# A hybrid decoder layer on one core: other costs in the kernel's own scheduler, a sixth side bank, and output rows turned in one operation

## The chip, the core and the metric

The kernel runs on one core of a Trainium2 chip. TensorE (PE) multiplies, VectorE (DVE) and ScalarE (ACT) work element by element, GpSimd (POOL) does a little, and SyncE (SP) issues nearly all DMAs. Every engine works through its own queue in order. A matmul adds into one of the eight PSUM banks, 128 partitions of 512 floats each. The time is device microseconds of one execution; what counts is the median of several runs.

## The reference

One layer for 256 new tokens of a prompt and 64 tokens of eight running sequences, all in float32:

```python
proj = x @ w_in                       # 2048 -> 16392 columns
(ml_q, ml_k, ml_v, ml_i, ml_f, ml_o, hg_q, hg_f, hg_i, hg_g, gate_a, gate_b) = split(proj)
h, C, n, m = mlstm(q, k, v, ig, lf, C0, n0, m0)      # 4 heads, state 256 x 512 each
branch_a = layernorm(h) * ml_norm_g * sigmoid(ml_o)
o, S = hgrn2(hq, log f, 1 - f, i, S0)                # 8 heads, state 128 x 256 each
branch_b = rmsnorm(o) * hg_norm_g * silu(hg_g)
merged = sigmoid(gate_a) * (branch_a @ w_branch_a) + sigmoid(gate_b) * (branch_b @ w_branch_b)
x1 = layernorm(alpha * x + merged @ w_out)
y = layernorm(alpha * x1 + relu(x1 @ w_up) ** 2 @ w_down)
```

The outputs are y for both groups and the new states of all heads (C, n, m of the mLSTM, S of the HGRN2).

## The kernel before

**The main stream.** All weight products are cut into tiles of 128 output columns for all 320 tokens. A tile sums 16 blocks of 128 rows (k). Each float32 factor is split into a high and a low part, so one k is three matmuls, which this document calls a step: high x high, high x low, low x high. A tile is 16 steps, 48 matmuls. The weights come in units of half a tile (eight blocks, 128 x 1024 floats): SP loads one (`wr<-wt`), ACT copies its high part (`wh`), DVE takes the low part (`wl`, in `prep`, L497). The list of tiles (`tile_list`) fixes the order of the main stream: for each of the four mLSTM heads v, k, q and two gates (the gates are `ga` and `gb`, the merge gates); four more gates; for each of the eight HGRN2 heads two gates, f, q and two tiles of i; 16 tiles of the mLSTM output gate (`o`), four gates, then 16 pairs of HGRN2 output gate and branch projection (`hg`, `wa`), `wb`, `wo`, and the feed-forward part (`up`, `dn`).

**The side work.** The heads' recurrences are written as generators (`m_E`, `m_S`, `m_V`, `m_num`, `m_sample`, `m_update`, ... for the mLSTM, `h_scan`, `h_i`, `h_state`, `h_out`, ... for the HGRN2). Each yields one instruction at a time with its engine and its cost, or waits for an event, or takes or returns a buffer from a pool. Their matmuls ("side matmuls") stand between the main ones.

**What sets the order.** The class `Sched` keeps an account: a time for every engine, counted in nanoseconds from given costs, not measured. After each step of the main stream (`run_main`) it lets the generators run as far as the account permits. An instruction may be written down if its input is ready by the account, plus a latency: LAT if it comes from another engine, SAME if it comes from the same one. A side matmul needs PE_LAT (450) more and is written only when the account's TensorE time has reached that point. So the numbers of the account decide where each instruction stands in its engine's queue; the time on the chip decides whether it then has to wait. A DMA counts 620 on SP, then 1,500 plus its bytes at 380 a nanosecond plus 600 (`transfer`). `until` lets the account's time pass until a condition holds.

**Banks.** Three of the eight banks serve the main stream (`mbank`), one the gates' first product and then, like the other four, the side work (`sbank`). A tile's evacuation (`ev_...`) returns its bank after its first reading; for gates and the `o` and `hf` tiles that reading is a DVE operation in `sigmoid` (L1309), for the others an ACT copy.

**Lines the text speaks of.** L356 is the helper of all matmuls that are not transposes, L350 that of all ACT operations, L359 that of all DMAs of SP. L1156 and L1159 are the turning transposes of DVE (`turn`, 24 for each head), L1631 that of the HGRN2's output rows, L1090 that of the mLSTM's. `h_i` turns i, splits it (L1488, tile `rh`) and multiplies it by a spreading matrix (`rh,ra`, two side matmuls of 128 x 256). `h_state` stacks k in two parts (`stack`, L987) and has TensorE transpose the result (L1530), from which ACT makes four copies of 32 partitions. `m_sample` multiplies the mLSTM states, loaded from HBM (`rx<-C`, `f<-C`, 16 loads of 256 KB for each head), in two groups of eight matmuls a head: eight groups in all; `m_update` and `m_store` change the states and store them (`Cs`). L1049 is the end of the mLSTM's layernorm (`ln_post`), whose rows TensorE transposes at L1212. `m_CP` stores k (`kD`, four DMAs of 32-partition pieces) and v (`vD`, 1 MB) for later use.

Of the kernel before, what the change touches and what calls it, by code (L numbers as in the profile page):

```python
# [20 lines left out]
TOK = 320  # L21
# [4 lines left out]
LN_SH = 62  # L26
# [93 lines left out]
V_MLG, V_HGG, V_G1, V_B1, V_G2, V_B2, V_LB, V_BI, V_BF, V_END = 0, 16, 32, 48, 64, 80, 96, 112, 113, 114  # L120


LAT = 140.0
SAME = 100.0
PE_LAT = 450.0


# [16 lines left out]
class Sched:  # L144
# [24 lines left out]
    def step(self, c, now):  # L169
        if c.req is None:  # L170
            try:
                c.req = c.gen.send(c.send)
            except StopIteration:
                c.done = True
                return False
            c.send = None
        kind = c.req[0]
        if kind == "wait":
            for e in c.req[1]:
                if e.t is None:  # L180
                    return False
            c.ready = max([c.ready] + [e.t for e in c.req[1]])
            c.eng = None
        elif kind == "acq":
            pool, n = c.req[1], c.req[2]
            if len(pool.free) < n:
                return False
            pool.free.sort(key=lambda x: x[0])
            got, pool.free = pool.free[:n], pool.free[n:]
            c.ready = max([c.ready] + [x[0] for x in got])  # L190
            c.eng = None
            c.send = got[0][1] if n == 1 else [x[1] for x in got]
        elif kind == "rel":
            c.req[1].free.append((c.ready, c.req[2]))
        elif kind == "set":
            c.req[1].t = c.ready
        else:
            _, cost, fn, *after = c.req
            r = max(after[0]) if after else c.ready
            if c.eng != kind or after:  # L200
                r += LAT
            elif kind in ("act", "dve"):
                r += SAME
            if kind == "pe":
# [62 lines left out]


def dve_t(n):
    return 155.0 + 1.07 * n  # L270


def pe_f(n, m=128):
# [40 lines left out]
class Program:  # L314
# [163 lines left out]
    def prep(self, must=False):  # L478

        u = self.next_prep  # L480
        if u >= len(UNITS) or not self.hl_free:
            return False
        now = self.s.t["pe"]
        if must:
            self.s.until(lambda: u in self.raw_at)
        elif u not in self.raw_at:
            return False
        if not must and (self.raw_at[u] > now + 200 or self.hl_free[0][0] > now + 200 or self.s.t["dve"] > now + 1200):
            return False
# [4 lines left out]
        e = s.use("act", max(at, self.raw_at[u]) + LAT, act(1024))  # L494
        self.A(hi, raw)
        e = s.use("dve", e + LAT, dve(1024))
# [85 lines left out]
    def before(self, i, t):  # L582
        s = self.s
        kind, h, c = t[:3]
        if kind == "mv" and c == 0:
            s.until(lambda: self.vr.free and self.qk.free)
            self.m_start(h)
            self.vr.free.sort(key=lambda x: x[0])
            self.mh[h]["vr"] = self.vr.free.pop(0)[1]
        elif kind == "hf":  # L590
            s.until(lambda: self.hs.free)
            if h == 0:
                s.spawn(self.m_after(), 0)
            self.h_start(h)
        elif kind == "o" and h == 0:
            s.until(lambda: all(m["end"].t is not None for m in self.mh))
        elif kind == "hg" and h == 0:
            s.until(lambda: all(m["end"].t is not None for m in self.hh))
            self.carve_m()
            self.carve_b()  # L600
            B = self.Part(self.f2)
            for pool in (self.sg, self.sg, self.sr, self.ld, self.ld, self.ld):
                pool.free.append((s.t["pe"], B(320)))
        if kind in ("o", "wa", "hg", "wb"):
            s.spawn(self.fetch(kind, h), 1)
        elif kind == "mk" and h == 0 and c == 0:
            self.load_ev.t = s.t["pe"]
            self.dma(self.lmask, self.d["lmask"])
        elif kind == "wo" and h == 0:
            s.until(lambda: len(self.sbank.free) >= 5)  # L610
            self.mbank.free += self.sbank.free[:3]
            del self.sbank.free[:3]
            self.hl_free += [(s.t["pe"], x) for x in self.wx[:4]]
            R = self.Part(self.wxv[4].rearrange("p x s v -> p (x s v)"))
            self.lns = [R.three(2, TOK) for _ in range(3)]
            s.spawn(self.ln_x(), 1)
        elif kind == "dn" and c == 3 and h == 0:
# [302 lines left out]
    def m_S(self, h):  # L920
# [20 lines left out]
        yield ("act", act(128), lambda: self.A(ss[64:128, 0:128], E[64:128, 384:512]))  # L941
# [361 lines left out]
    def sigmoid(self, p, out, r, free=()):  # L1303
# [9 lines left out]
        yield ("act", act(TOK), lambda: self.A(r, out, AF.Ln, scale=2.0 ** -LN_SH, bias=self.ln_b))  # L1313
        yield ("act", act(TOK), lambda: self.A(r, r, AF.Exp, scale=-1.0, bias=self.exp_b))
        yield ("dve", dve(TOK), lambda: v.scalar_tensor_tensor(out, out, 1.0, r, ALU.add, ALU.mult))  # L1315
        yield ("dve", dve(TOK), lambda: v.scalar_tensor_tensor(out, out, 2.0, r, ALU.subtract, ALU.mult))  # L1316

    def ev_hf(self, h, c, b):
# [5 lines left out]
        yield ("act", act(TOK), lambda: self.A(u, f, AF.Identity, scale=-1.0, bias=self.one))  # L1324
        yield post(m["fd"])

    def ev_hq(self, h, c, b):
# [109 lines left out]
    def h_lag(self, b, at):  # L1437
        v = self.nc.vector
        a4 = at[:, 0:TOK].rearrange("p (b r) -> p b r", r=4)
        for d in (0, 2, 1, 3):  # L1440
# [4 lines left out]
            yield ("dve", dve(n, True), lambda: v.copy_predicated(  # L1445
                a4[:, :, d:4], block(self.lmask[:, M_LAG[d]:M_LAG[d] + n]), block(x[:, lo:lo + n])))
            if d > 1:
                yield rel(self.sbank, x)
# [1 line left out]
    def h_put(self, b, at, B):  # L1450
# [3 lines left out]
        elif B >= 32:  # L1454
            for j in range(64 // B):
                for i in range(2):
                    lo, c = 64 * j + B * i, 128 * i + 64 * j
                    yield ("act", act(B, True), lambda: self.A(
                        at[64 * j:64 * j + B, c + B:c + 2 * B], b[lo:lo + B, c // 2:c // 2 + B]))
        else:  # L1460
            T = TOK if B == 4 else NP_
# [51 lines left out]
    def h_state(self, h):  # L1513
# [17 lines left out]
        yield rel(self.hstg, st)  # L1531
        for x in range(4):
            r = slice(32 * x, 32 * x + 32)
            yield ("act", act(256, True), lambda: self.A(kst[r, x], b[r, 0:256].rearrange("p (g k) -> p g k", g=2)))
        yield rel(self.sbank, b)
        ob = yield acq(self.sbank)
        m["ob2"] = ob
# [77 lines left out]
    def h_out(self, h):  # L1615
# [11 lines left out]
        for i in range(2):  # L1627
            yield from self.rms(b[:, 256 * i:256 * i + 256], on[:, i, :], 128)
        yield rel(self.sbank, b)
        for i in range(2):  # L1630
            yield ("dve", dve_t(256), lambda: v.transpose(on[:, i, :], on[:, i, :]))  # L1631
# [59 lines left out]
    def ev_o(self, j, c, b):  # L1691
# [5 lines left out]
        x = yield from self.fetched("o", j)  # L1697
        yield ("dve", dve(TOK, ptr=1), lambda: v.scalar_tensor_tensor(g, g, self.vec[:, V_MLG + j:V_MLG + j + 1], x, ALU.mult, ALU.mult))  # L1698
        yield rel(self.ld, x)
        yield from self.split(g, self.bah[:, j, :], self.bal[:, j, :])  # L1700
        yield rel(self.sg, g)
        yield post(self.ba_ev[j])
# [386 lines left out]
```

## Time and profile before

| | |
|---|---|
| median of 3 runs | 2305.03 us (2302.9 to 2306.02) |
| profiled execution | 2302.73 us |
| its span | 2300.8 us |
| granted TensorE clock | 0.999 |
| busy share PE / DVE / ACT / POOL | 100% / 63% / 45% / 1% |
| moved by DMA | 424.94 MB, mean 185 GB/s |

The page puts 69% of the chain that ended last down to TensorE. The ends of matmuls are modelled: a main matmul of 320 columns is shown as 0.31 us long, though the next one starts about 0.15 us after it. A gap shorter than that overlap is not shown as idle. Where TensorE waits for a moment, the starts of consecutive matmuls tell more than the busy time. A name like `rx<-C` is output from input; numbers of buffers are left out.

### The profile page before, as it was taken

What the parts mean: (1) busy time and instruction counts of PE and PEld (TensorE: products, weight loads), DVE (VectorE), ACT (ScalarE), POOL (GpSimd) and SP (SyncE); (2) the same over time, 40 slices, a digit from 0 to 9 for tenths busy, and PEclk for the clock granted to TensorE, in tenths of its full rate; (3) what the DMA queues carried; (4) which work ended last, traced back from release to release, by engine and by line L of the source; (5) the groups of instructions that cost most, each with busy time, mean ns of one, the idle gap of its engine ahead of it and who ended that gap; (6) DMA issues with size and microseconds to landing.
All of it is one profiled execution on the core that took longest, in us unless ns stands there. A gap on an engine that the chain in (4) does not pass through costs nothing.

```text
span 2300.8 us, 38921 instructions
## 1 busy us (share of the span) xinstructions
PE 2289.6 (100%) x15592; PEld 2246.1 (98%) x15592; DVE 1458.9 (63%) x2634; ACT 1036.6 (45%) x1653; POOL 13.5 (1%) x37
## 2 busy tenths in 40 slices
PE   9999999999999999999999999999999999999998
PEld 9999899999999999999999999999999999999998
DVE  6786786788888886555555767654444444444455
ACT  5443445455555565444433446533433343234334
POOL 0000000000000000000000000000000000000000
PEclk9999999999999999999999999999999999999999
DMA  7667977755565564555545644444444444444475
GB/s 284 211 186 259 295 250 229 259 176 185 191 207 187 166 198 167 180 174 170 176 172 175 214 163 147 147 147 149 154 147 150 152 147 153 149 147 154 149 228 193
DMA packets 214574, 424.94 MB, mean 185 GB/s; under 512 B 83572, under 2 KB 110068, under 8 KB 213368
## 3 DMA queue, kind: packets, MB, share of 16 engines
q1 hardware_dynamic: 209512, 415.97, 53.7%
q0 software_dynamic: 4736, 6.29, 1.0%
q8 instruction: 122, 2.00, 0.3%
q14 instruction: 60, 0.49, 0.1%
q10 hardware_dynamic: 144, 0.20, 0.0%
HBM read 371.48 MB, written 50.90 MB: 184 GB/s over the span
## 4 chain that ended last, share of the span: by engine, by line
PE 69%; DVE 3%; ACT 1%; issue 0%; ACTq 0%; DVEq 0%
PE bank L356 69%; DVE wl L497 1%; ACT wh L350 0%; DVE f L1156 0%; DVE f L1445 0%; ACT f L350 0%; DVE f3m L1973 0%; DVE f3m L1980 0%; ACT f3m L350 0%; DVE f L1159 0%; DVE f L1315 0%; DVE f L1316 0%; DVE f L1631 0%; DVE f L1698 0%; DVE f L1309 0%
## 5 line engine op out<-in xcount | busy, mean ns | idle before, releaser
L356 PE MATMUL bank<-xh,wh 128*128 128x320 f32 (+1 forms) x2504 | 794.6, 318 | 0.0
L356 PE MATMUL bank<-xh,wl 128*128 128x320 f32 (+1 forms) x2504 | 774.8, 310 | 0.0
L356 PE MATMUL bank<-xl,wh 128*128 128x320 f32 (+1 forms) x2504 | 772.2, 309 | 0.0
L497 DVE TENSOR_TENSOR wl<-wr,wh 128x1024 fp32r<-128x1024 f32 x440 | 538.7, 1224 | 361.4 <-ACT wh L350 358.3
L350 ACT ACTIVATE wh<-wr 128x1024 fp32r<-128x1024 f32 x440 | 465.4, 1058 | 524.7 <-PE bank L356 495.6
L356 PEld LDWEIGHTS bank<-xh,wh 128*128 128x128 f32 x2504 | 472.0, 189 | 17.2 <-issue 15.3
L356 PEld LDWEIGHTS bank<-xl,wh 128*128 128x128 f32 x2504 | 471.5, 188 | 3.3
L356 PEld LDWEIGHTS bank<-xh,wl 128*128 128x128 f32 x2504 | 471.8, 189 | 0.2 <-DVE wl L497 0.2
L497 DVE TENSOR_TENSOR bb<-wr,bb 128x1024 fp32r<-128x1024 f32 x162 | 198.5, 1225 | 193.7 <-ACT bb L350 193.5
L350 ACT ACTIVATE bb<-wr 128x1024 fp32r<-128x1024 f32 x162 | 171.6, 1059 | 294.6 <-PE bank L356 277.5
L356 PE MATMUL bank<-ra,wh 128*128 128x320 f32 x1008 | 275.9, 309 | 0.7 <-DVE ra L1672 0.7
L356 PE MATMUL bank<-ra,bb 128*128 128x320 f32 x1096 | 255.2, 309 | 0.0
L356 PE MATMUL bank<-xh,bb 128*128 128x320 f32 (+1 forms) x1136 | 253.8, 309 | 0.0
L356 PE MATMUL bank<-rxb,bb 128*128 128x320 f32 x1088 | 249.0, 309 | 0.0
L356 PEld LDWEIGHTS bank<-xh,bb 128*128 128x128 f32 x1136 | 191.0, 188 | 0.0
L356 PE MATMUL bank<-rxb,wh 128*128 128x320 f32 x608 | 187.5, 308 | 0.0
L356 PE MATMUL bank<-rxb,wl 128*128 128x320 f32 x608 | 187.5, 308 | 0.0
L356 PEld LDWEIGHTS bank<-ra,bb 128*128 128x128 f32 x1096 | 184.9, 187 | 0.0
L356 PEld LDWEIGHTS bank<-rxb,bb 128*128 128x128 f32 x1088 | 184.2, 187 | 0.0
L356 PEld LDWEIGHTS bank<-ra,wh 128*128 128x128 f32 x1008 | 180.9, 187 | 0.9 <-DVE ra L1672 0.9
L356 PE MATMUL bank<-xl,bb 128*128 128x320 f32 (+1 forms) x568 | 175.5, 309 | 0.0
L356 PE MATMUL bank<-bb,wh 128*128 128x320 f32 (+1 forms) x536 | 119.0, 313 | 0.0
(259 smaller groups left out, 2244.4 us busy)
## 6 DMA issues: line engine op xcount, KB each, us to landing
wr<-wt SPq DMA_DIRECT2D x602, 512.0 KB, 3.3
rx<-C SPq DMA_DIRECT2D x34, 256.0 KB, 5.6
Cs<-rx SPq DMA_DIRECT2D x34, 256.0 KB, 4.8
f<-C SPq DMA_DIRECT2D x30, 256.0 KB, 5.5
Cs<-f SPq DMA_DIRECT2D x30, 256.0 KB, 4.1
f<-first SPq DMA_DIRECT2D x6, 704.0 KB, 9.6
vD<-ra SPq DMA_DIRECT2D x4, 1024.0 KB, 5.2
f<-S SPq DMA_DIRECT2D x8, 512.0 KB, 5.0
```

Of the source, the lines that this page charges most:

```text
L350: return self.nc.scalar.activation(out, in_, func, **kw)
L356: self.nc.tensor.matmul(*a, **kw)
L497: self.V().tensor_tensor(lo, raw, hi.bitcast(F32), ALU.subtract)
```

## The change

LAT falls from 140 to 130. SAME, 100 for ACT and DVE, becomes 127 for ACT and 113 for DVE. A result of TensorE counts 200 until another engine can use it (PE_OUT) instead of LAT. A DVE transpose of n elements counts 295 + 1.05 n instead of 155 + 1.07 n. An ACT copy from or to part of the partitions counts 122 more (PART), at four places. ACT operations with a pointer operand count 93 more at three places. The masked copies of `h_lag`, 398, 315, 231 and 148 before, get fixed costs of 415, 385, 320 and 155. The weight split counts 10 to 20 more.

From the tile `mk` of the first head on, one main bank goes to the side work, which then has six; before the first `hg` tile it goes back. In `h_out` one transpose of 512 columns takes the place of two of 256. In `ev_o` the tiles from the eighth on wait in the account for the last HGRN2 head's attention matrix (`aT`), those from the thirteenth on for its states (`sdone`), ahead of their split.

```diff
-LAT = 140.0
-SAME = 100.0
+LAT = 130.0
+SAME = dict(act=127.0, dve=113.0)
+PE_OUT = 200.0
+PART = 122.0
...
             r = max(after[0]) if after else c.ready
-            if c.eng != kind or after:
+            if c.eng == "pe" and kind != "pe" and not after:
+                r += PE_OUT
+            elif c.eng != kind or after:
                 r += LAT
-            elif kind in ("act", "dve"):
-                r += SAME
+            elif kind in SAME:
+                r += SAME[kind]
...
 def dve_t(n):
-    return 155.0 + 1.07 * n
+    return 295.0 + 1.05 * n
...
+            self.mbank.free.append(self.sbank.free.pop())
             B = self.Part(self.f2)
...
         elif kind == "mk" and h == 0 and c == 0:
+            s.until(lambda: self.mbank.free)
+            self.sbank.free.append(self.mbank.free.pop())
             self.load_ev.t = s.t["pe"]
...
-            yield ("act", act(256, True), lambda: self.A(kst[r, x], b[r, 0:256].rearrange("p (g k) -> p g k", g=2)))
+            yield ("act", act(256, True) + PART, lambda: self.A(kst[r, x], b[r, 0:256].rearrange("p (g k) -> p g k", g=2)))
...
-        for i in range(2):
-            yield ("dve", dve_t(256), lambda: v.transpose(on[:, i, :], on[:, i, :]))
+        yield ("dve", dve_t(512), lambda: v.transpose(on[:, 0:2, :], on[:, 0:2, :]))
...
         yield rel(self.ld, x)
+        if j > 6:
+            yield wait(self.hh[HH - 1]["aT" if j < 12 else "sdone"])
         yield from self.split(g, self.bah[:, j, :], self.bal[:, j, :])
```

The main stream is the same, step for step, and so are the 681 side matmuls; what moves is where they stand. Two places show it. Lines are numbered four to eight higher in the new kernel: L497, L987, L1156, L1159, L1418, L1419 are now L501, L994, L1163, L1166, L1425, L1426.

First DVE's queue in the fourth HGRN2 head, before: from one weight split to the end of the stacking (L987), with the turning of i (L1156) and the norm of the head before (L1664, L1056) between them.

```order
L497 TENSOR_TENSOR wl<-wr,wh 128x1024
L1419 TENSOR_TENSOR f_75<-f_75 128x40
L1156 STREAM_TRANSPOSE f_76<-f_75 32x4x32
L1466 COPY_PREDICATED f_75<-lmask,bank_88 128x40x4
L1156 STREAM_TRANSPOSE f_76<-f_75 32x4x32
L1664 TENSOR_SCALAR misc<-misc 128x1
L1056 TENSOR_SCALAR misc<-misc 128x1
L1156 STREAM_TRANSPOSE f_76<-f_75 32x4x32
L987 TENSOR_TENSOR f_76<-f_75,f_76 128x16x8
```

The same stretch now, from the split of the same unit to the stacking of the same head:

```order
L501 TENSOR_TENSOR wl<-wr,wh 128x1024
L1425 TENSOR_TENSOR f_75<-f_75 128x16x8
L1166 STREAM_TRANSPOSE f_76<-f_75 32x2x32
L994 TENSOR_TENSOR f_76<-f_75,f_76 128x16x8
L1426 TENSOR_TENSOR f_75<-f_75 128x16
```

Seven rows stood between the split and the stacking, now two do; the transposes of TensorE that read the result (L1530) stand at the 1,163rd step before and at the 1,161st now.

Then SP's queue ahead of the fifth group of state matmuls (the third mLSTM head's first). `rx<-C` loads states, `Cs` stores them, `vD` and `kD` are the stores of `m_CP`, `gaD` that of a gate. Before:

```order
L359 DMA gaD_160<-f_76 128x320
L359 DMA Cs<-rx 128x512
L359 DMA vD_114<-ra 128x2048
L359 DMA wr<-wt 128x1024
L359 DMA Cs<-rx 128x512
L359 DMA rx<-C 128x512
L359 DMA Cs<-rx 128x512
L359 DMA rx<-C 128x512
```

Now:

```order
L363 DMA Cs<-rx 128x512
L363 DMA rx<-C 128x512
L363 DMA wr<-wt 128x1024
L363 DMA rx<-C 128x512
L363 DMA Cs<-rx 128x512 x2
L363 DMA wr<-wt 128x1024
L363 DMA rx<-C 128x512 x2
L363 DMA gaD_159<-f_76 128x320
```

The 1 MB store of v no longer stands close ahead of the group's last two loads. Ahead of the third group it is now so with kD, which before stood farther off:

```order
L363 DMA gaD_158<-f_76 128x320
L363 DMA kD_109<-ra 32x32x32
L363 DMA Cs<-rx 128x512
L363 DMA rx<-C 128x512
L363 DMA vD_113<-ra 128x2048
```

Here the `rx<-C` is the group's last load, behind the last of kD's four stores. All eight groups, in both versions, stand on TensorE within 50 steps of each other's place.

More of the change, by code (lines that the diff above doesn't have):

```diff
@@ L493, in prep @@
         s = self.s
-        e = s.use("act", max(at, self.raw_at[u]) + LAT, act(1024))
+        e = s.use("act", max(at, self.raw_at[u]) + LAT, act(1048))
         self.A(hi, raw)
-        e = s.use("dve", e + LAT, dve(1024))
+        e = s.use("dve", e + LAT, dve(1034))
         self.V().tensor_tensor(lo, raw, hi.bitcast(F32), ALU.subtract)
@@ L940, in m_S @@
         yield ("act", act(384), lambda: self.A(sh, E[:, 0:384]))
[L941 removed]
+        yield ("act", act(128) + PART, lambda: self.A(ss[64:128, 0:128], E[64:128, 384:512]))
         yield ("dve", dve(384), lambda: v.tensor_tensor(sl, E[:, 0:384], f(sh), ALU.subtract))
@@ L1312, in sigmoid @@
         yield ("act", act(TOK), lambda: self.A(out, out, AF.Exp))
-        yield ("act", act(TOK), lambda: self.A(r, out, AF.Ln, scale=2.0 ** -LN_SH, bias=self.ln_b))
-        yield ("act", act(TOK), lambda: self.A(r, r, AF.Exp, scale=-1.0, bias=self.exp_b))
+        yield ("act", act(TOK, False, 1), lambda: self.A(r, out, AF.Ln, scale=2.0 ** -LN_SH, bias=self.ln_b))
+        yield ("act", act(TOK, False, 1), lambda: self.A(r, r, AF.Exp, scale=-1.0, bias=self.exp_b))
         yield ("dve", dve(TOK), lambda: v.scalar_tensor_tensor(out, out, 1.0, r, ALU.add, ALU.mult))
@@ L1323, in ev_hf @@
         yield ("dve", dve(TOK, mode=2), lambda: v.tensor_scalar(f, u, l1, lb, ALU.mult, ALU.add))
-        yield ("act", act(TOK), lambda: self.A(u, f, AF.Identity, scale=-1.0, bias=self.one))
+        yield ("act", act(TOK, False, 1), lambda: self.A(u, f, AF.Identity, scale=-1.0, bias=self.one))
         yield post(m["fd"])
@@ L1444, in h_lag @@
             block = lambda y: y.rearrange("p (b r) -> p b r", r=4 - d)
-            yield ("dve", dve(n, True), lambda: v.copy_predicated(
+            yield ("dve", (415.0, 385.0, 320.0, 155.0)[d], lambda: v.copy_predicated(
                 a4[:, :, d:4], block(self.lmask[:, M_LAG[d]:M_LAG[d] + n]), block(x[:, lo:lo + n])))
@@ L1457, in h_put @@
                     lo, c = 64 * j + B * i, 128 * i + 64 * j
-                    yield ("act", act(B, True), lambda: self.A(
+                    yield ("act", act(B, True) + PART, lambda: self.A(
                         at[64 * j:64 * j + B, c + B:c + 2 * B], b[lo:lo + B, c // 2:c // 2 + B]))
```

## The prediction

> **What bounds the kernel now.** I read the page first, then the windows by stage, the waits of TensorE and its timeline around each wait. The page says that TensorE has work all the time:
>
> ```profile
> span 2300.8 us, 38921 instructions
> PE 2289.6 (100%) x15592; PEld 2246.1 (98%) x15592; DVE 1458.9 (63%) x2634; ACT 1036.6 (45%) x1653; POOL 13.5 (1%) x37
> ```
>
> This profiled execution took 2302.73 us, 1.9 more than its span and 2.3 less than the median of the three runs, 2305.03; the sum is made against 2302.73 and carried over to the median as a difference. The windows (PE busy and its matmuls in brackets, then weight loads, DVE, ACT, POOL, granted clock, DMA share, GB/s) give the pace:
>
> ```profile
> 30.00:430.00 400.00, 399.07 (x2690) 371.86 (x2689) 306.09 (x620) 179.27 (x293) 0.00 (x0) 1.00 0.75 245
> 430.00:830.00 400.00, 397.37 (x2781) 386.69 (x2781) 339.54 (x899) 224.17 (x490) 4.74 (x13) 1.00 0.59 190
> 830.00:2277.00 1447.00, 1446.34 (x9853) 1445.61 (x9852) 781.29 (x1042) 599.20 (x802) 5.90 (x8) 1.00 0.48 163
> ```
>
> From 830 to 2277 us a matmul starts every 1447/9853 = 0.147 us at full clock: nothing but fewer matmuls helps there. The first two windows hold the mLSTM and HGRN2 heads, whose side matmuls go between the main ones. The change removes no matmul, so all it can win or lose is TensorE's waiting. The waits (total, times, longest):
>
> ```profile
> PE bank L1530 <- DVE f L987: 1.5, 3, 0.7
> PE bank L356 <- DVE rh L1488: 1.1, 2, 0.6
> PE bank L356 <- POOL ones L640: 1.0, 1, 1.0
> PE bank L1212 <- DVE f L1049: 0.7, 1, 0.7
> PE bank L356 <- DVE ra L1672: 0.7, 1, 0.7
> PE bank L356 <- DMA rx<-C: 0.2, 1, 0.2
> ```
>
> L640 is the start, L1672 lies at 1493 us in the feed-forward part. The other four rows, seven waits, lie in the two windows of the heads. They cost more than is printed, because a matmul counts as busy for 0.31 us but the next starts after 0.147. The timeline of TensorE shows it; the first three rows have a wait, the last three the same matmul without one:
>
> ```profile
> 603.36 0.30 PE L356 MATMUL bank<-xh,wl 128*128 128x320 f32 x1
> 604.33 0.33 PE L1530 MATMUL bank<-cst,f 128*128 128x128 f32 x1 [0.67 <-DVE f L987]
> 604.42 0.39 PE L356 MATMUL bank<-xh,wh 128*128 128x320 f32 x1
> ...
> 605.23 0.31 PE L356 MATMUL bank<-xh,wl 128*128 128x320 f32 x1
> 605.38 0.27 PE L1530 MATMUL bank<-cst,f 128*128 128x128 f32 x1
> 605.41 0.39 PE L356 MATMUL bank<-xh,wh 128*128 128x320 f32 x1
> ```
>
> From main matmul to main matmul it is 1.06 us against 0.18: the 0.67 cost 0.88. So the six waits for DVE, 1.5 + 1.1 + 0.7 = 3.3 printed, cost 3.3 + 6 x 0.21 = 4.6 us. Groups of eight matmuls on the mLSTM states, loaded just ahead of them, differ in the same way:
>
> ```profile
> 232.13 0.31 PE L356 MATMUL bank<-xh,wl 128*128 128x320 f32 x1
> ...
> 234.22 0.42 PE L356 MATMUL bank<-xh,wh 128*128 128x320 f32 x1
> ...
> 265.80 0.31 PE L356 MATMUL bank<-xh,wl 128*128 128x320 f32 x1
> ...
> 268.18 1.05 PE L356 MATMUL bank<-rx,f 128*32 128x512 f32 x2 [0.22 <-DMA rx<-C]
> ...
> 269.15 0.41 PE L356 MATMUL bank<-xh,wh 128*128 128x320 f32 x1
> ...
> 179.83 0.31 PE L356 MATMUL bank<-xh,wl 128*128 128x320 f32 x1
> ...
> 182.72 0.41 PE L356 MATMUL bank<-xh,wh 128*128 128x320 f32 x1
> ...
> 814.72 0.31 PE L356 MATMUL bank<-xh,wl 128*128 128x320 f32 x1
> ...
> 815.13 0.31 PE L356 MATMUL bank<-xh,wh 128*128 128x320 f32 x1
> ...
> 816.10 0.31 PE L356 MATMUL bank<-xh,wl 128*128 128x320 f32 x1
> ...
> 816.37 0.31 PE L356 MATMUL bank<-xh,wh 128*128 128x320 f32 x1
> ```
>
> A group without a wait takes 2.09 us, the one with the printed wait 3.35 (1.26 lost), the one at 180 us 2.89 (0.80 lost, not printed). There are seven such unprinted losses, from the 0.80 here to 0.14 at 814.72 (0.41 against the 0.27 at 816.10 around the same side matmul, one for L1488's tile), together 2.4 us: 1.25 on two state groups, 1.15 on five waits for DVE or ACT. In all the heads lose 5.75 us to computing that comes late and 2.5 to states that come late: 8.25 us, 0.36% of the time. That is all there is to win.
>
> **The change part by part.** A difference under 0.2%, 4.6 us, is about what a measurement of this kernel cannot tell from none.
>
> *The numbers of the account.* They move side work, and no engine gets or loses an instruction by them. TensorE waited at 604.33 for L987, which stood in DVE's queue behind transposes:
>
> ```profile
> 602.27 0.31 DVE L1156 STREAM_TRANSPOSE f<-f 32x128 f32<-32x128 f32 x1
> 602.59 0.33 DVE L1466 COPY_PREDICATED f<-lmask,bank 128x160 f32<-128x160 uint8 x1
> ...
> 603.99 0.29 DVE L987 TENSOR_TENSOR f<-f,f 128x128 fp32r<-128x128 f32 x1
> ```
>
> A transpose of 128 takes the queue 0.32 us there; the old account says 155 + 1.07 x 128 = 292 ns, the new one 429. By groups:
>
> ```profile
> L1156 DVE STREAM_TRANSPOSE f<-f 32x128 f32<-32x128 f32 x96 | 29.0, 303 | 2.3
> L1631 DVE STREAM_TRANSPOSE f<-f 128x256 f32<-128x256 f32 x16 | 7.0, 435 | 0.0
> L1090 DVE STREAM_TRANSPOSE f<-f 128x512 f32<-128x512 f32 x8 | 5.7, 709 | 0.2
> L350 ACT ACTIVATE ra<-bank 32x256 fp32r<-32x256 f32 x32 | 12.0, 374 | 5.5 <-PE bank L1530 5.1
> ```
>
> The old account was short by little in each and by much in sum: a head's 24 turning transposes, and 264 ns for each of four partial copies that take 374. The new one is long instead (429, 564 and 833 for 303, 435 and 709; 386 for 374), about 3.3 us more for a head's turning, while the longest wait for DVE cost some 0.9 (0.7 printed + 0.21). DVE will so be ahead of the account, not behind. The order shows it at head 3: of seven rows between a split and L987 two are left, which at 0.2 to 0.33 a row is some 1.3 us earlier, while its transposes on TensorE stay within two steps of their place. The gain is between 0 (the waits only move) and 5.75. I take 4.6: the six printed waits go, and the five small ones, no longer than the account's own steps, come back elsewhere.
>
> *Side work earlier, then later.* Counted along the main matmuls, mLSTM's side work moves 20 to 50 steps earlier (a step is three matmuls, 0.44 us) and the last HGRN2 heads' 20 to 130 later; the 681 side matmuls are the same. With them move, on SP's queue, the loads and stores of states and the small stores; POOL's order is as before. The later heads end at the 1,692nd step, 100 steps (44 us) before the first tile of the HGRN2 output gate, which needs them: hidden, and priced 0. Were that cover gone, each step over would cost 0.44 us.
>
> *The loads of states.* This is what the account still leaves out. SP issued the last load of the group that waited at 268.18 here:
>
> ```profile
> 262.34 0.42 SPq L359 DMA_DIRECT2D rx<-C  x1
> ...
> rx<-C SPq DMA_DIRECT2D x34, 256.0 KB, 5.6
> vD<-ra SPq DMA_DIRECT2D x4, 1024.0 KB, 5.2
> ```
>
> Issue to use was 5.84 us, the median landing 5.6; the account gives 620 for the issue, 2,790 for the transfer and 580 to TensorE, 3.99 us, in both versions. Two of the three state groups that waited, at 180 and 268 us, have the 1 MB store of vD and the scattered stores of kD among their last loads on SP. In the new order the fifth group (268 us) is rid of them, and two other groups, the third and the seventh, have their last load right behind kD's stores. The bounds: 0, and seven groups that each wait 5.84 - 3.99 = 1.85 us, 13.0. I take 2 x 1.26 for the two, 0.45 for one and 0.2 for the rest, 3.2 against 2.5: 0.7 us lost; it is nearest to what the same neighbours cost now.
> By the Trainium skill (DMA: Bandwidth & Descriptors, Anatomy of one DMA) a transfer takes 2.0 us plus its bytes at 436 GB/s, for 262,144 bytes an estimate of 2.6 us. The median landing here is 5.6, so the trace does not agree while stores run beside. By that page no load would be late, the 3.2 would be 0, and the sum would come to -7.1 us instead of -3.9.
>
> *The sixth side bank.* From the fifth tile to the HGRN2 output gate the main stream has two banks, not three. A tile's bank must then be emptied while the next tile runs, 48 x 0.147 = 7.06 us. The slowest emptying now, from the tile's last matmul to the start of the read:
>
> ```profile
> 539.65 0.31 PE L356 MATMUL bank<-xh,wl 128*128 128x320 f32 x1
> ...
> 542.60 0.48 DVE L1309 TENSOR_SCALAR f<-bank 128x320 f32<-128x320 f32 x1
> ```
>
> That is 3.4 us with the read; it could double. Along ACT's order all 56 emptyings keep their place among the weight splits, along DVE's all but a few within one split. Price 0; if not hidden, each microsecond over 7.06 is one lost.
>
> *Output rows turned in one operation.* Eight of 709 ns for sixteen of 435: DVE is busy 1.3 us less, beside TensorE, whose waits above name L987, L1488 and L1049, never L1631. It could hold another DVE row up by 709 - 435 = 0.27 us longer, 2.2 over eight heads, or shorten a wait as much; I take 0.
>
> *The wait for the last head (in ev_o).* It holds two side buffers, not an engine. The order has that head's last attention matmul at step 1,603 and the first tile that waits ends at step 1,600: a hold of two or three steps, which two free banks (14 us) hide. Behind the output gate the engines' orders are the same but for bank numbers and one copy at the end, at most one 0.48-us row; 0. L1672's wait stays.
>
> The sum: -4.6 + 0.7 = -3.9 us, 2298.8 for the profiled execution, 2305.03 - 3.9 = 2301 for the median.
>
> **The rivals.**
> Waits that only change place: for it speaks that the account's margin to TensorE (450 ns) is unchanged, against it that its DVE is now long rather than short. Time 2305, within 2.
> The loads come in time too: -4.6 - 2.5 = -7.1, 2298. For it speaks that five of the eight state groups ran freely; against it the 5.6 us to landing. It is also what the page of the Trainium skill cited above would make of it.
> Slower, the state loads: if mLSTM's work, now earlier, puts every load directly ahead of its use, all seven groups behind the first wait 1.85 us: 13.0 - 2.5 - 4.6 = +5.9, 2311. It decides against the change from (4.6 + 2.5 + 4.6)/7 = 1.7 us a group. For it: in most groups the last load stands some steps nearer to its use on TensorE. Against: of the eight groups of now only two lost more than 0.5 us.
> Slower, the two banks: one emptying in each of eight heads at 8.2 us, 1.1 too late, costs 9 us, 2310; the longest of now is 3.4.
> That the order would not change is excluded by the order itself.
>
> **How the numbers follow.** The forecast (0.64) spans 2298.5 to 2303.5, by the five small waits, 1.15 us either way, and the loads, 0 to 2.4 more; nearly half of it lies beyond the bound at 2300.4, so 0.30 faster and 0.34 same. Waits that move 0.15, same. Loads in time too 0.08, faster. State loads 0.10 and two banks 0.03, slower. So faster 0.38, same 0.49, slower 0.13. The range 2296.5 to 2307 leaves out the slower rivals and a little of the fastest.
>
> **What would show it.** TensorE's waits should lose L987, L1488 and L1049 (now seven lines further down) to under 1 us in all, and keep rx<-C or f<-C at one to three places of over 1 us between main matmuls, before 430 us. The window from 830 to 2277 should keep its pace of 0.147 us. I am wrong if waits of DVE's small rows stay above 3 us, if a main matmul waits for L1309's successor or an ACT copy at a tile's start, or if a state group takes more than 4 us.

## The result: 0.35% faster, 0.8 us below the range

| | before | after |
|---|---|---|
| median | 2304.46 us (7 runs, 2302.65 to 2306.02) | 2295.66 us (7 runs, 2294.86 to 2297.23) |
| ratio | | 0.9965 (95%: 0.9956 to 0.9975) |
| profiled execution | 2302.73 us | 2296.11 us |

The medians lie 8.8 us apart, the two profiled executions 6.6. The head of the page after, then the same three windows as before (PE busy and its matmuls, weight loads, DVE, ACT, POOL, clock, DMA share, GB/s):

```profile
span 2294.3 us, 38944 instructions
PE 2285.9 (100%) x15592; PEld 2245.2 (98%) x15592; DVE 1458.0 (64%) x2626; ACT 1036.4 (45%) x1653; POOL 13.4 (1%) x37
```

```profile
30.00:430.00 400.00, 399.47 (x2702) 373.73 (x2701) 308.60 (x630) 180.24 (x297) 2.47 (x7) 1.00 0.78 250
430.00:830.00 400.00, 400.00 (x2805) 392.42 (x2804) 338.04 (x875) 225.32 (x481) 2.20 (x6) 1.00 0.59 187
830.00:2277.00 1447.00, 1446.34 (x9843) 1443.29 (x9842) 783.28 (x1060) 600.39 (x814) 5.89 (x8) 1.00 0.50 164
```

DVE has eight operations less, the output rows turned at once. In the window of the HGRN2 heads PE now has no idle time, and 24 more matmuls start in it. Counted in the traces, TensorE runs 904 side matmuls for the heads in both kernels; the 681 named ahead of this section is not a count of the traces. The third window has the old pace. The waits of TensorE after (total, times, longest) are all of them:

```profile
PE bank L360 <- POOL ones L647: 1.0, 1, 1.0
PE bank L360 <- DVE ra L1678: 0.7, 1, 0.7
PE bank L360 <- DVE ra L971: 0.5, 1, 0.5
```

The first two are those of L640 and L1672 of before. L994, L1495 and L1056, the lines on which six waits of before stood (there L987, L1488 and L1049), are gone. What is left is one new wait, 0.53 us printed and 0.8 lost against the same matmul without it, and state groups that still come late:

```profile
91.41 0.30 PE L360 MATMUL bank<-xh,wl 128*128 128x320 f32 x1
92.25 0.50 PE L360 MATMUL bank<-ra 128*128 128x512 f32 x1 [0.53 <-DVE ra L971]
92.59 0.31 PE L360 MATMUL bank<-xh,wh 128*128 128x320 f32 x1
...
380.60 0.31 PE L360 MATMUL bank<-xh,wl 128*128 128x320 f32 x1
...
383.61 0.41 PE L360 MATMUL bank<-xh,wh 128*128 128x320 f32 x1
```

The last group takes 383.61 - 380.60 = 3.01 us from main to main, 0.9 more than the clean 2.09.

**Where the time went.** In each trace I took, for every run of side matmuls, the time from the main matmul ahead to the fourth one behind, less 0.1467 us for each main matmul. What the kinds of side matmuls cost without a wait was fitted over all 18 traces; nothing then lies more than 0.03 us under the fit. What is over it by more than 0.1 us is counted as lost, an estimate that rests on the fit. Taken from a run's profiled time, these losses leave 2293.4 to 2295.0 us in all 18, so they account for nearly all the differences below. Lost, in us:

| | mLSTM state groups | computing, mLSTM | computing, HGRN2 | sum |
|---|---|---|---|---|
| before | 2.6 | 1.1 | 4.9 | 8.6 |
| after | 1.4 | 0.8 | 0.25 | 2.4 |

That is 6.2 of the 6.6 us; the first 200 main matmuls took 34.50 us after and 34.95 before, which is the rest (34.3 to 35.1 in the other traces).

### The profile page after: what moved, and what is told of

The parts are those of the page before. It is cut to its first block, busy times and chain, and to the rows that moved or that the text cites. A ratio compares the mean times of both kernels' runs of the same rounds, so it can differ in the third digit from the quotient of the medians.

```text
span 2294.3 us, 38944 instructions
## 1 busy us (share of the span) xinstructions
PE 2285.9 (100%) x15592; PEld 2245.2 (98%) x15592; DVE 1458.0 (64%) x2626; ACT 1036.4 (45%) x1653; POOL 13.4 (1%) x37
## 4 chain that ended last, share of the span: by engine, by line
PE 98%; DVE 1%; ACT 1%; issue 0%; DMA 0%; ACTq 0%; DVEq 0%
PE bank L360 97%; DVE f3m L1981 0%; DVE f3m L1988 0%; ACT wh L354 0%; DVE wl L501 0%; DMA f<-first 0%; ACT f L354 0%; ACT f3m L354 0%; PE bank L1034 0%; DVE f L1163 0%; PE bank L1537 0%; PE bank L1219 0%; PE bank L1647 0%; ACT xh L354 0%; DVE ra L971 0%
## 5 line engine op out<-in xcount | busy, mean ns | idle before, releaser
L501 DVE TENSOR_TENSOR wl<-wr,wh 128x1024 fp32r<-128x1024 f32 x440 | 538.8, 1225 | 367.0 <-ACT wh L354 364.7
L501 DVE TENSOR_TENSOR bb<-wr,bb 128x1024 fp32r<-128x1024 f32 x162 | 198.5, 1225 | 194.2 <-ACT bb L354 193.9
```

## Experiments

Losses as above, then the time of the profiled execution and the median, in us; the ratio is to runs of the kernel before on the same chip. "Cost" is that of a transpose in the account.

| run | cost | side banks | groups | mLSTM | HGRN2 | profiled | median | ratio (95%) |
|---|---|---|---|---|---|---|---|---|
| e1 before again | old | 5 | 3.2 | 1.1 | 4.9 | 2304.14 | 2304.11 | 1.0001 (0.9991 to 1.0011) |
| e2 numbers | new | 5 | 4.1 | 0.8 | 0.5 | 2299.51 | 2299.72 | 0.9984 (0.9975 to 0.9993) |
| e3 bank | old | 6 | 2.6 | 1.8 | 5.7 | 2303.74 | 2303.69 | 0.9998 (0.9989 to 1.0007) |
| e4 rows | old | 5 | 3.6 | 1.1 | 5.4 | 2304.39 | 2304.39 | 1.0003 (0.9994 to 1.0012) |
| e5 five banks | new | 5 | 5.4 | 0.8 | 5.4 | 2305.37 | 2304.01 | 1.0001 (0.9992 to 1.0010) |
| e6 old cost | old | 6 | 2.2 | 2.5 | 3.5 | 2301.88 | 2303.36 | 0.9998 (0.9989 to 1.0007) |
| e7 cost alone | new | 5 | 9.7 | 1.1 | 1.1 | 2306.01 | 2301.53 | 0.9990 (0.9982 to 0.9999) |
| e8 after, late loads | new | 6 | 0.0 | 0.8 | 0.3 | 2294.90 | 2295.21 | 0.9965 (0.9952 to 0.9979) |
| e9 before, late loads | old | 5 | 0.9 | 0.4 | 1.9 | 2297.45 | 2297.28 | 0.9970 (0.9959 to 0.9982) |
| e10 cost and bank | new | 6 | 0.4 | 1.6 | 0.4 | 2296.19 | 2296.58 | 0.9967 (0.9955 to 0.9979) |
| e11 after again | new | 6 | 1.3 | 0.8 | 0.3 | 2296.11 | 2296.29 | 0.9966 (0.9954 to 0.9979) |
| e12 late loads, scores | new | 6 | 0.0 | 0.8 | 0.3 | 2295.28 | 2295.28 | 0.9962 (0.9949 to 0.9974) |
| e13 before, loads +1000 | old | 5 | 1.2 | 0.0 | 2.9 | 2297.62 | 2297.96 | 0.9974 (0.9964 to 0.9984) |
| e14 before, loads +3000 | old | 5 | 0.1 | 0.4 | 3.3 | 2297.43 | 2297.43 | 0.9970 (0.9959 to 0.9981) |
| e15 before, loads +4000 | old | 5 | 0.1 | 0.5 | 4.6 | 2298.63 | 2299.41 | 0.9980 (0.9971 to 0.9989) |
| e16 after, loads +3000 | new | 6 | 0.1 | 1.9 | 0.1 | 2296.10 | 2296.21 | 0.9968 (0.9956 to 0.9981) |

### e1: the kernel before once more

No edit.

> The kernel before, unchanged, for a second trace of it. If the waits for DVE's small rows belong to the order of the instructions, the same six come back (L987, L1488 and L1049, 3.3 us printed in the first trace, within 0.5). If the losses at the state groups depend on how the transfers happen to land, they differ from the 1.26 us, 0.80 us and 0.45 us of the first trace, by up to 2 us in all: the medians of before and after lie 8.8 us apart, the two profiled executions only 6.6, and this would be the 2.2 between them. If the whole of it is fixed by the order, the losses are the same to 0.3 us.

The waits of TensorE in its trace:

```profile
PE bank L1530 <- DVE f L987: 1.3, 2, 0.6
PE bank L356 <- DVE rh L1488: 1.1, 2, 0.6
...
PE bank L1212 <- DVE f L1049: 0.7, 1, 0.7
PE bank L356 <- DMA rx<-C: 0.7, 1, 0.7
...
PE bank L1530 <- DVE misc L1664: 0.2, 1, 0.2
```

The waits for computing stand at the same places and lose the same 6.0 us in both traces; the state groups lose 3.2 instead of 2.6. The eighth group, at 405 us, lost 1.7 here and 0.45 before; the third 0.4 and 0.8. So in these two executions the order fixed what was lost in computing, and what the state groups lost was drawn anew. It was not SP's queue that made the difference at the eighth group. SP issued its last two loads 4.2 us ahead of the main matmul in front of the group (405.92) in the first trace, and 4.3 us ahead (405.19) in this one:

```profile
401.68 0.90 SPq L359 DMA_DIRECT2D rx<-C  x2
400.86 0.99 SPq L359 DMA_DIRECT2D rx<-C  x2
```

(SPq is SP's queue.) With the same lead the group lost 0.45 and 1.7 us: what differed was how long the loads took to land.

### e2, e3, e4: each part alone

e2 has every new number of the account (LAT, SAME, PE_OUT, PART, `dve_t`, pointers, masked copies), and nothing else. e3 has only the two moves of a bank:

```diff
+            self.mbank.free.append(self.sbank.free.pop())
...
+            s.until(lambda: self.mbank.free)
+            self.sbank.free.append(self.mbank.free.pop())
```

e4 has only the one transpose of 512 and the wait in `ev_o`. e2 leaves that wait out, and its y and HGRN2 states come out wrong: its order is so late that, by the code, the mLSTM output gate's split overwrites memory which the last HGRN2 head still reads. Its engines carry out the same work, so its time is used here.

> The kernel before with the account's new numbers alone: five side banks, two transposes for the output rows, no wait in ev_o. Theory A, the numbers carry it: 2295 to 2298 us, TensorE's waits for L987, L1488 and L1049 (some lines further down) under 1 us in total. Theory B, the sixth side bank carries a good part, because side work no longer stands back for a bank: 2299 to 2302 us and at least two of the six waits left. Theory C, the order of before was one unlucky draw among many and any other order loses less: somewhere between 2294 and 2302, with waits at other places.

> The kernel before with the sixth side bank alone. Theory A: 2303 to 2306 us, 3 us or more of waits for DVE's small rows as before, though maybe at other places. Theory B: 2299 to 2302 us. Theory C: a new order too, so 2294 to 2302. All three: no main matmul waits for the emptying of a bank; if one does, the two main banks have a price.

> The kernel before with the output rows turned in one operation and the wait in ev_o, and nothing else. Theories A and B: 2303 to 2306 us, DVE's busy time 1.3 us less, the waits for DVE's small rows still 3 us or more. Theory C: 2294 to 2302, since here too the order changes.

TensorE's waits in e2, from 30 to 430 us; from 430 to 830 its window has no idle time:

```profile
PE bank L360 <- DMA rx<-C: 1.9, 2, 1.1
PE bank L360 <- DVE ra L968: 0.5, 1, 0.5
```

And in e3, for the whole span, the rows at the head (L990 and L1491 are L987 and L1488, L1644 is L1641):

```profile
PE bank L1644 <- ACT f L350: 1.2, 5, 0.3
...
PE bank L1030 <- DVE f L990: 0.7, 1, 0.7
...
PE bank L356 <- DVE rh L1491: 0.4, 1, 0.4
PE bank L1533 <- DVE f L990: 0.4, 2, 0.2
```

The numbers alone take most of the waits for computing away (6.0 us to 1.3), as theory A had it, but the state groups come later (2.6 to 4.1), so that half of the gain is left; the time, 2299.7, is above theory A's range. The bank alone and the rows alone give nothing, though both make another order: theory C, as far as these two go, gets no support. No main matmul of e3 waits for the emptying of a bank in the heads' part: no price of two main banks is seen.

### e5, e6, e7: what the gain needs

e5 is the new kernel without the two moves of a bank, e6 the new kernel with

```diff
-    return 295.0 + 1.05 * n
+    return 155.0 + 1.07 * n
```

and e7 the kernel before with the reverse of that edit and the wait in `ev_o`.

> The new kernel with five side banks, that is without the change of banks, all else as it is there. The trace of the numbers alone had no wait left for DVE's small rows but 4.0 us lost at two state groups (182 and 267 us), where before lost 2.5 and after 1.4. Theory A2, the numbers remove the waits for computing, and the bank only shuffles which state groups come late: computing loses under 1.5 us, the state groups 3 to 4 us, 2298 to 2300. Theory B2, the bank itself shortens the side work: waits for DVE or ACT of 2 us or more come back, 2298 to 2301.

> The new kernel with a transpose counted as 155 + 1.07 n again. If it is the transposes that the old account had short (the prediction's reading), TensorE waits again for L994, L1495 or L1056, 3 us or more in computing, 2298 to 2302. If TensorE's result at 200, the partial copies and the latencies carry it, computing loses under 1.5 us and the time is 2294 to 2298, with the state groups deciding where.

> The kernel before with the transposes counted as 295 + 1.05 n and the wait in ev_o, nothing else. If the transposes carry it: computing loses under 2 us instead of 5.75, 2298 to 2301. If they are one number of several: 3 to 5 us still lost, 2301 to 2304.

e5 was a surprise: it is as slow as before, at 2304.0. Its waits for computing stayed away, except at one place that no theory had. TensorE there, at the mLSTM's output gate:

```profile
856.97 0.31 PE L360 MATMUL bank<-xh,wl 128*128 128x320 f32 x1
857.11 0.41 PE L360 MATMUL bank<-f,f3h 128*128 128x128 f32 x2
857.45 1.07 PE L360 MATMUL bank<-f3h 128*32 128x256 f32 x16
...
860.57 0.67 PE L360 MATMUL bank<-f,f 128*128 128x256 f32 x2
863.11 0.64 PE L360 MATMUL bank<-xh,wh 128*128 128x320 f32 x1 [1.88 <-DVE f L1313]
```

For 6.1 us no main matmul stands here, and 4.9 of them are lost: the gate's tiles wait in `ev_o` for the last head's attention matrix, hold the side buffers, the banks are not emptied (L1313 is L1309, the first reading of such a tile), and the scheduler places the head's remaining work without main matmuls between. What seems to count is where that head's attention product stands: at the 1,664th step in e5, at the 1,603rd in the new kernel. In e2 it stands later still (1,720th), but there nothing waits for it. e7, below, has the wait, five banks and the new cost, and its heads end as late as e5's (step 1,759 against 1,756); its attention product stands at the 1,653rd step, and nothing is lost to the hold. So the 4.9 us look like an edge that e5 just crosses, not like a price of five banks and the new cost as such. The state groups of e5 lose 5.4. The bank, worth nothing by itself, is worth 8 us here, and without the other numbers, in e7 against e10, which has the rows too and ran on another chip, 5 us by the medians: with it the heads' work ends earlier (step 1,692 in the new kernel), and the state groups lose less in every trace that has it beside the new cost.

In e6, with all but the transposes' cost, the waits on L994 and its like come back, and 5.9 us are lost in computing. Its median, 2303.4, is that of the kernel before, and slower than either theory had it:

```profile
PE bank L360 <- DVE rx L1278: 0.7, 2, 0.6
...
PE bank L1537 <- DVE f L994: 0.6, 2, 0.4
PE bank L360 <- DMA f<-C: 0.5, 1, 0.5
PE bank L1647 <- ACT f L354: 0.4, 1, 0.4
PE bank L1219 <- DVE f L1056: 0.4, 1, 0.4
```

In e7, with that cost alone, they are gone (2.15 us lost in computing, half of it just behind its latest state group), but the groups lose 9.7 us in the profiled execution, which was the slowest of its 11 (2297.9 to 2306.0). It shows how a group comes late: SP's queue ahead of the last group of the mLSTM, then what SP waited for from 378 to 386.5 us, then TensorE's wait:

```profile
378.28 0.43 SPq L359 DMA_DIRECT2D wr<-wt  x1
383.90 0.34 SPq L359 DMA_DIRECT2D rx<-C  x1
384.33 0.65 SPq L359 DMA_DIRECT2D Cs<-rx  x1
385.07 0.38 SPq L359 DMA_DIRECT2D gaD<-f  x1
385.55 0.44 SPq L359 DMA_DIRECT2D rx<-C  x1
```

```profile
SPq L359 <- DMA Cs<-rx: 5.1, 1, 5.1
```

```profile
384.89 1.91 PE L356 MATMUL bank<-f 128*32 128x512 f32 x12
387.45 1.05 PE L356 MATMUL bank<-rx,f 128*32 128x512 f32 x2 [0.65 <-DMA rx<-C]
390.88 1.91 PE L356 MATMUL bank<-rx,f 128*32 128x512 f32 x2 [2.39 <-DMA rx<-C]
```

The load uses the buffer of a state that is being stored. SP stands 5.1 us until the store has landed, and the last load goes out at 385.55, after TensorE has begun the group. The account lands the store, too, 2.8 us after its issue. In e2, SP waited in the same way, 4.8 and 5.2 us in all, in the 12 us ahead of the two groups that came late there.

### e8, e11, e12: the new kernel's own rest

e8 and e12 have, after the load of a state,

```diff
-            m["parts"][n].t = t
+            m["parts"][n].t = t + 2000.0
```

and e12 also 115 more for the scores' product in `m_S`; e11 is the new kernel unchanged.

> The new kernel, with each load of an mLSTM state counted as landing 2,000 ns later than before in the account. If the state groups lose what is left because the account lands their loads too early, all eight groups run in 2.09 us, no wait on rx<-C or f<-C stays, and the time falls by the 1.4 us lost there in the trace of after, to 2293.5 to 2295. If holding the groups back only makes the states' buffers free later, so that the next loads come later too, the groups still lose 1 us or more, and the time stays at 2295 to 2297.

> The new kernel unchanged, for a second trace. The losses in computing (0.8 us at 91 us, 0.2 at 821) come back to 0.1 us; the state groups at 345 and 381 us lose something else than 0.46 and 0.91, if they depend on the landing, and the groups that lost nothing lose nothing again where their slack was over 1 us. 2295 to 2297.

> The new kernel with the state loads counted 2,000 ns later, and with the product of the mLSTM's scores with the decay matrix (DVE, 384 columns, one operand from a bank) counted as 580 ns, its time in the trace, instead of 465. If the wait of 0.8 us at 91 us comes from that short cost, it goes, and the time is 2294 to 2295, 0.5 to 1 us under the new kernel with late states alone. If the new order puts another small wait in its place, 2295 to 2296.

In e8 the last group, first and last main matmul around it:

```profile
382.17 0.31 PE L360 MATMUL bank<-xh,wl 128*128 128x320 f32 x1
...
384.26 0.41 PE L360 MATMUL bank<-xh,wh 128*128 128x320 f32 x1
```

2.09 us, and so in all eight. The 1.4 us of the state groups are gone from the trace, as the first theory had it. The medians say less: 2295.21 and 2295.28 against 2295.66 and 2296.29 for the new kernel, with overlapping intervals of the ratios, so that a gain over it is not shown by time; the nearest hint is e12 against e11 on one chip, 1.0 us between the medians of five runs each, with one run of e12 among e11's. e11 drew 0.5, 0.4 and 0.4 us at the groups of 346, 178 and 381 us, where the first trace had 0.5, 0 and 0.9. The wait at 91 us stayed at 0.81 in e12: the scores' cost is not its cause.

### e9, e13, e14, e15, e16, e10: cost or luck

e9 and e13 to e15 are the kernel before with 2,000, 1,000, 3,000 and 4,000 in that line, e16 the new kernel with 3,000. e10 is the kernel before with the transposes' new cost, the bank, the rows and the wait in `ev_o`; all other numbers are old. In e15, which lacks the wait and whose heads end at the 1,772nd step, part of the HGRN2 states that it writes are not the reference's, as in e2.

> The kernel before, with each load of an mLSTM state counted as landing 2,000 ns later in the account, nothing else. If the account's early landing is what costs at the state groups, none of the eight loses over 0.2 us (2.5 and 3.1 us in the two traces of before), the waits for DVE and ACT stay (5 to 7 us in computing), and the time is 2300 to 2302, with runs closer together than the 5 us of before. Rival: the order is so shaken that computing waits take the place, 2303 to 2306.

> The new kernel with only the transposes' new cost, the sixth bank, the output rows and the wait in ev_o; the latencies, TensorE's result at 200, the partial copies, the pointers and the masked copies as before. If the transposes were the one number that was short by enough, computing loses under 2 us and the time is 2295 to 2299. If the other numbers are needed as well, 3 to 5 us are lost in computing, on ACT's small copies and on the masked copies, and the time is 2299 to 2303.

> The kernel before with the state loads counted 1,000 ns later. If the old cost of the transposes is what makes TensorE wait, and 2.4 us with loads 2,000 later was a lucky order, computing loses 4 to 7 us again, the state groups about 1, 2298 to 2301. If the later loads themselves relieve the waits for computing, or any order but the first is as good, computing loses under 3 us and the time is 2296 to 2298.

> The kernel before with the state loads counted 3,000 ns later. By the transposes' cost: computing loses 4 to 7 us, the state groups under 0.5, 2297 to 2300. By later loads or by the draw: computing under 3 us, 2295 to 2297.

> The kernel before with the state loads counted 4,000 ns later. By the transposes' cost: computing loses 4 to 7 us, the state groups under 0.5, 2297 to 2300. By later loads or by the draw: computing under 3 us, 2295 to 2297.

> The new kernel with the state loads counted 3,000 ns later. By the transposes' cost: computing loses 1 to 2 us in this order too, as in seven orders with the new cost so far, the state groups under 0.2, 2294 to 2296. By the draw: anything from 1 to 6 us in computing, up to 2300.

e9 gave a second surprise. One line in the kernel before, and the time is 2297.3, most of the whole change's gain. The groups gained 1.7 to 2.3 us, nearly as expected: seven of the eight lost nothing, but one lost 0.9 where none was to lose over 0.2, and the time is below the 2300 to 2302 expected. But computing fell from 6.0 to 2.3 as well, with the old cost. Three more orders with the old cost, made to decide between the cost and a lucky order, lost 2.9, 3.6 and 5.1 in computing. By what was expected of them this is one for luck or the later loads (e13), one between (e14) and one for the cost (e15): as totals they do not decide. A split by stage, made after these totals were seen, tells more. In the HGRN2 heads, which have most of the turning, eight orders with the old cost lost 1.9 to 5.7 us, and six with the new one (after, e2, e5, e7, e10, e16) 0.1 to 1.1, leaving out e5's hold. e8 and e12 lost 0.3 but are no further orders: at least 98% of their side matmuls in these heads stand where the kernel after has them. The two sets do not overlap; e6 and e10 differ in this cost and in the other numbers, and show the same. In the mLSTM part old (0.0 to 2.5) and new (0.8 to 1.9) do overlap: there it is a draw, the luck of the order.

This shows that the longer count of a transpose takes the waits away there. It does not show that the old count was too short. The old formula gives 292, 429 and 703 ns for 128, 256 and 512 columns, and by the rows of the profile before they took 303, 435 and 709; at 603 us one of 128 held DVE's queue for 0.32 us. The new formula gives 429, 564 and 833. So it may be the room that the account now leaves on DVE that counts, and not its truth: a count of what a transpose takes, or the same room given to other operations, was not tried.

e10 also says that beside cost, bank, rows and wait the other numbers of the account are worth nothing that can be seen: 2296.58 against 2296.29 for the new kernel on the same chip (e11).

e16's waits, after the one at the start, show what such a draw looks like, a wait on L994 in the mLSTM that the kernel after does not have:

```profile
PE bank L1034 <- DVE f L994: 0.7, 1, 0.7
PE bank L360 <- DVE ra L1678: 0.7, 1, 0.7
PE bank L360 <- DVE ra L971: 0.5, 1, 0.5
```

Why all four orders with later loads lost less in the HGRN2 than before (1.9 to 4.6 against 4.9) is not settled: it can be four draws, or that the heads' work stands some 30 to 130 steps later.

## Why the prediction was wrong

Its sign was right, but it had the median fall by 3.9 us, and it fell by more than twice that. Its sum was 2.7 us short for the profiled execution, most of it in the loads of states, which it had at +0.7 and which measured -1.2; carrying the sum to the median added as much again.

- **What bounds, and what can be won.** Right. The third window kept 0.147 us, L1672's wait stayed. The losses came out as 8.6 us where the prediction had 8.25; beside them only the start gained, 0.45.
- **The numbers of the account, -4.6.** Right in size: computing lost 6.0 us before and 1.05 after, -4.9. All six printed waits went, and "the five small ones come back elsewhere" was one wait of 0.8 and one of 0.2. That the rest came so near the 1.15 that the prediction left is in part luck: other orders with the new cost lost 1.3 to 2.15. That the count of the transposes does it is shown for the HGRN2 by e6, e7 and e10. That the old count was short "by much in sum" is not: it gave 292 ns for 128 columns and 223 for 64, where they took 303 and 238, and 24 such differences are 0.3 us a head; the new count is longer than the operations are. And the prediction credited the numbers alone with the gain; without the sixth bank the later order gives half of it back in e2, and all of it in e5.
- **The sixth side bank, 0, and the wait in ev_o, 0.** Each holds by itself: e3 measured 0.9998, e4 1.0003, no emptying showed, and the hold of two or three steps cost nothing. The step asked only what the bank could cost, by the two main banks. It never asked what the order would be without it, where the runs show 5 to 8 us.
- **The loads of states, +0.7.** This is the term that failed: measured -1.2 (2.6 to 1.4; e1 against e11: 3.2 to 1.3). The places were half right: the fifth group ran freely, the seventh lost 0.5, the third, priced at 1.26, lost 0 and 0.4, and the eighth, which got no more than the 0.45 that it lost before, 0.9 and 0.4. The prediction took the worst group's price for the two groups whose last load goes out right behind the stores of k; the third lost 0 and 0.4, the seventh 0.5 and 0.5, so that place in the queue does not set the price. Two other causes show: in e7's queue a load goes out late because the store that holds its buffer lands late; at e1's eighth group the loads go out as early as before and land later. Which of them made the groups of the new order cheaper than before is open. The median landings after, 4.6 for the loads into `rx` (5.6 before) and 4.9 for their stores, are both far over the account's 2.8:

```profile
rx<-C SPq DMA_DIRECT2D x34, 256.0 KB, 4.6
Cs<-rx SPq DMA_DIRECT2D x34, 256.0 KB, 4.9
```

- **The rival with the loads in time.** Its sum, -7.1, is nearest to the 6.6 of the profiled executions, but not by its mechanism: 1.4 us is still lost at the groups. The Trainium skill (DMA: Bandwidth & Descriptors, Anatomy of one DMA) makes 2.6 us of a 256 KB transfer, an estimate from its two figures, which the page fitted to DMAs that GpSimd issues; these are SP's. The trace does not agree for the loads of states: those into `rx` took 4.6 here, and in e8, with 2 us more than the account's 2.8, no group was late. For the 512 KB weight loads the same two figures make 3.2 us, again an estimate, and there the trace agrees:

```profile
wr<-wt SPq DMA_DIRECT2D x602, 512.0 KB, 3.3
```

Most of these run where no states move; from 30 to 430 us, where they do, the weight loads whose landing is recorded took 4.3.
- **From the profiled execution to the median, +2.3.** Wrong. The prediction moved the sum by 2305.03 - 2302.73 as if that difference were the kernel's. 27 and 33 further runs of before had medians of 2303.78 and 2303.64; the profiled one was a quick one, and e1's trace shows 0.6 us of the difference at the state groups. After, the median lies 0.45 us below the profiled execution. With the measured terms the sum for the profiled execution is -4.9 - 1.2 - 0.5 (start) = -6.6; the 1.9 missed at the loads, 0.3 in computing, 0.5 at the start, the 2.3 carried over and this 0.45 are, but for rounding, the 5.3 us between 2301 and 2295.66.
- **The slower rivals.** Neither came. State loads that come late are what e5 and e7 have, 5.4 and 9.7 us in their profiled executions, at about half of the eight groups and not at all of them: the mechanism was real where the bank was missing. In e5 it and the hold together ate the whole gain; e7 kept 0.1%.
- **Chances.** 0.49 on no measurable difference came from a forecast that lay just inside the bound; with the loads' sign right it would have lain outside.

## What to carry to other kernels

Where a scheduler's account writes the order, look which operation stands in front of the waits again and again, and count it longer: here that one number brought the waits for computing in the HGRN2 heads from 4.9 us to 1.1 or less in every order tried but the one with the hold. Whether its true time would have done is not shown. A longer cost also makes the work later, so look whether buffers, banks and deadlines behind it still hold, and try the parts together: here cost, bank and rows each gave less than 0.2% alone, and the cost and the bank together, with the rows and the wait that guards the last head, all of it. There was another way to most of it: counting the loads of states 2 us later, and nothing else, gave 0.30% (e9). Count a transfer in such an account as it lands beside other traffic, and the store that frees a load's buffer with it.

## What was not expected of the hardware

Waits for computing came back to within 0.05 us from one execution to the next, while one and the same state group lost 0.45 us in one and 1.7 in another. Runs of a kernel spread over 2301.3 to 2306.3 in 33 runs of before and 2297.9 to 2306.0 in 11 of e7. That the groups cause this spread is not shown: 5 runs of e8, which has no late group, lie between 2294.8 and 2296.6, and 5 of e11, which has three, between 2296.0 and 2296.8. A 256 KB store that frees a buffer held SP's whole queue for 5.1 us in e7.
